# Gate and up projections: the low part of every second weight block made by an accumulating transfer instead of VectorE

## The chip, the cores and the metric

One core of one Trainium2 chip runs the whole program. The metric is the device time of one execution in microseconds (us). Lower is better.

## The reference, cut to what matters

The program is a decoder of two layers in float32 on 256 tokens of width 2048. Each layer has a mixer (retention and block attention) and a feed-forward part. The change touches only the first line of the feed-forward part and its product with the up projection:

```python
def conv_ffn(h, w_gate, w_up, conv_w, conv_b, w_down):
    a = h @ w_gate                       # 256 x 2048 times 2048 x 5632
    ...
    for j in range(CONV_WIDTH):
        conv = conv + conv_w[j] * a_pad[:, j:j + S]
    return (jax.nn.silu(conv) * (h @ w_up)) @ w_down
```

Everything is float32 outside and the result must keep that precision, so a product of two float32 matrices is made from parts: each operand is split into a high part (rounded to the type float32r that TensorE takes) and a low part (what the rounding left, again in float32r), and the products high by high, high by low and low by high are added up in PSUM.

## The kernel before, in words

All weights of both layers (428 MB) are read once, as a stream of 816 blocks, in a fixed order written out by hand (`units`). A block is 512 KB: two row tiles of 128 rows by 512 columns (or one row tile by 1024 columns). Each block goes through three steps.

- `load(i)` (line 552) has SyncE's queue (SP) bring the block from HBM into a tile `wraw`, of which there are 4.
- `prepare(i)` (line 561) makes the two parts: ScalarE (ACT) copies `wraw` into `whi`, which rounds it (line 56), and then VectorE (DVE) subtracts `whi` from `wraw` into `wlo` (line 57). There are 3 tiles `whi` and 3 tiles `wlo`, used in turn: block i takes the tiles of block i-3.
- `multiply(i)` (line 567) has TensorE (PE) do the block's matmuls.

The main loop puts them in order on the engines: in round i it issues `load(i+3)`, `prepare(i+2)` and then `multiply(i)`, and after that the small steps that are due (`slots`). Since the instructions of an engine run in the order in which they are issued, ACT's copy for block i+2 stands before the small steps of round i and after those of round i-1.

A block of the gate or up projection has the mode `ws4`. It is 8 pairs of matmuls, for two row tiles and four groups of 128 columns: the high part of the weights with both parts of the activations (512 columns, line 597), and the low part of the weights with the high part of the activations (256 columns, line 598). So the low part is wanted by the second matmul of a block. There are 176 such blocks in each layer, 8 to a chunk of 512 columns, gate and up chunks in turn. The small steps beside them are the convolution's taps and the gated product (`ffn_gate`, `ffn_up`): ACT, DVE and GpSimd (POOL) each have a few, the only ones on POOL being `sr` (line 463) and a tiny memset (line 448).

The other transfers that POOL's queue issues in the kernel are small parameters at the start and `dec` (line 236), a table of 768 KB, once in each layer.

Of the kernel before, what the change touches and what calls it, by code (L numbers as in the profile page):

```python
# [12 lines left out]
AF = mybir.ActivationFunctionType  # L13
OP = mybir.AluOpType
AX = mybir.AxisListType

P = 128
# [9 lines left out]
NC = 512  # L27
UK = 2
# [5 lines left out]
def trunk(ctx, tc, x, ln1_g, w_in, ret_norm_g, q_norm_g, k_norm_g, w_out, ln2_g,  # L34
          w_gate, w_up, conv_w, conv_b, w_down, decay, dneg, out):
    nc = tc.nc
    pe, act, dve, pool = nc.tensor, nc.scalar, nc.vector, nc.gpsimd
# [12 lines left out]
    def f(ap):  # L50
        return ap.bitcast(F32)

    def split(hi, lo, src, scale=None):
        """hi + lo == src * scale exactly, each in the tensor engine's float32r."""
        if scale is None:
            act.activation(hi, src, AF.Copy)  # L56
            dve.tensor_tensor(lo, src, f(hi), op=OP.subtract)  # L57
        else:
            act.activation(hi, src, AF.Copy, scale=scale)
            dve.scalar_tensor_tensor(lo, src, scale, f(hi), op0=OP.mult, op1=OP.subtract)  # L60
# [9 lines left out]
        pe.matmul(o, a_hi, b_lo, start=False, stop=False, **kw)  # L70
        pe.matmul(o, a_lo, b_hi, start=False, stop=last, **kw)  # L71

    # ---- constants, parameters by feature on the partitions
    xs = const.tile([P, 2, D], F32, name="xs")
    ident = const.tile([P, P], F32, name="ident")
    make_identity(nc, ident)
# [2 lines left out]
    rows = [[] for _ in range(6)]  # L79
# [33 lines left out]
    def pcol(t, at):  # L113
        return par[:, t, at:at + 1]

    # ---- the stream of weight blocks: UK tiles of 128 rows, 512 columns
    units = []
    slots = {}
    pre = {}
# [6 lines left out]
        slots.setdefault(i, []).append((fn, a))  # L126

    def chunk(w, col, kts, lhs, mode, done):
        """kts: pairs (row tile of w, key of lhs); lhs(key) -> [P, 2, 256] hi and lo."""
        box = {}  # L130
        n = len(kts)
        step = 1 if mode == "wm2" else UK
        for u in range(0, n, step):
            units.append((w, kts[u][0], col, lhs, [k for _, k in kts[u:u + step]], mode,
                          box, u == 0, u + step >= n, done))
# [11 lines left out]
    def g_of(k):  # L147
        return gT["t"][:, k]

    # ---- norm of x by 512 columns: transposed and split, the row factor left to later  # L150
    def finalize(c, l, which):
        add, last = fin_acc.pop("acc", None), l == L
        cs = slice(c * NC, (c + 1) * NC)
        if add is not None:
            for t in range(2):
                dve.tensor_tensor(xs[:, t, cs], add[t], xs[:, t, cs], op=OP.add)
                if last:
                    nc.sync.dma_start(xout[:, t, cs], xs[:, t, cs])
        if last:
            return  # L160
        for t in range(2):
            act.activation(junk, xs[:, t, cs], AF.Square, accum_out=ssx[:, t, c:c + 1])
# [22 lines left out]
    row = {}  # L185
# [37 lines left out]
                        norm_tail(l, which)  # L223
        return fn

    # ---- attention
    A = {}

    def open_attention():
# [11 lines left out]
    def moba_qk(l, hc, which):  # L241
        def fn(acc):
# [29 lines left out]
            def turn():  # L272
                T = A["p"].tile([P, 4, 2, S], F32R, tag=f"{which}T", name=f"{which}T")
                A[which, "T"] = T
                g = pcol(5, (gq_at if which == "q" else gk_at) + l)
                for b in range(2):
                    pt = bank().rearrange("p (k t) -> p k t", k=2)
                    for hh in range(2):
                        for t in range(2):
                            pe.transpose(pt[:, hh, t * P:(t + 1) * P], raw[:, t, 2 * b + hh], ident)  # L280
                    split(T[:, 2 * b:2 * b + 2, 0], T[:, 2 * b:2 * b + 2, 1], pt, g)
# [6 lines left out]
    def v_done(key):  # L288
        def fn(acc):
            v = A["p"].tile([P, 2, 2, NC], F32R, tag=key, name=key)  # L290
            A[key] = v
            for t in range(2):
                split(v[:, t, 0], v[:, t, 1], acc[t], row["r"][:, t:t + 1])
        return fn
# [125 lines left out]
        split_all([(y[:, 2 * h + kk, 0], y[:, 2 * h + kk, 1], pt[:, kk], pcol(5, gr_at + 8 * l + 2 * h + kk))  # L420
                   for kk in range(2)])

    # ---- feed-forward
    FFN = {}

    def open_ffn():
# [75 lines left out]
                later(i, tile_of, i)  # L502
        return fn

    # ---- the order of it all
    kd = [(k, k) for k in range(KD)]
    for l in range(L):
        b = len(units)
# [4 lines left out]
        for hc in range(2):  # L513
            o = hc * NC
            chunk(W, MQ + o, kd, h_of, "wm", moba_qk(l, hc, "q"))
            chunk(W, MK + o, kd, h_of, "wm", moba_qk(l, hc, "k"))
            chunk(W, MV + o, kd, h_of, "wm", v_done("mv"))
            chunk(W, RK + o, kd, h_of, "ws2", ret_qk("rk"))
            chunk(W, RQ + o, kd, h_of, "ws2", ret_qk("rq"))
            chunk(W, RV + o, kd, h_of, "wm", v_done("rv"))  # L520
            chunk(W, RG + o, kd, h_of, "wm", gate_done)
            for i in range(4):
                at_unit(b + (3 + 7 * hc) * U + 2 + 6 * i, moba_head, 4 * hc + i)
            e = b + (6 + 7 * hc) * U
            for i in range(2):
                h = 2 * hc + i
                at_unit(e + 1 + 3 * i, ret_scores, h)
                at_unit(e + 3 + 3 * i, ret_values, h)
                at_unit(e + 8 + 2 * i, ret_gate, h)
                at_unit(e + 9 + 2 * i, ret_turn, l, h)  # L530
# [19 lines left out]
    raws, parts = {}, {}  # L550
# [10 lines left out]
    def prepare(i):  # L561
        hi = wpool.tile([P, UK, NC], F32R, tag="whi", name="whi")
        lo = wpool.tile([P, UK, NC], F32R, tag="wlo", name="wlo")
        split(hi, lo, raws.pop(i))
        parts[i] = hi, lo

    def multiply(i):
# [39 lines left out]
    n = len(units)  # L607
# [11 lines left out]
    params([0])  # L619
    transposed(0, 0, 1)  # L620
    prepare(0)
    transposed(1, 0, 1)
    prepared = 1
# [11 lines left out]
    for i in range(n):  # L635
        now[0] = i
        for fn in pre.get(i, []):
            fn()
        load_to(i + 4)
        while prepared < min(n, i + 3):  # L640
            prepare(prepared)
            prepared += 1
        multiply(i)
        for fn, a in slots.pop(i, []):
            fn(*a)
# [46 lines left out]
```

## Time and profile before

| what | value |
| --- | --- |
| median time | 2386.4 us (2 runs, 2386.07 to 2386.74) |
| span of the profiled execution | 2387.3 us |
| PE busy | 2371.1 us (99%) |
| DVE busy | 1439.0 us (60%) |
| ACT busy | 1160.7 us (49%) |
| POOL busy | 179.9 us (8%) |
| moved by DMA | 436.14 MB, 183 GB/s over the span |

The span runs from the first to the last instruction of one execution. For the profiled execution no other time is recorded than its span; it is 0.9 us (0.04%) above the median of the unprofiled runs, and so the two are taken as one. Busy time is the time in which at least one instruction of the engine ran. Matmuls overlap, so a busy PE isn't a PE at its peak.

### The profile page before, as it was taken

The page shows a single profiled execution, that of the slowest core. Times are in us where ns is not written, and L with a number is a line of the kernel's source. Part 1 is how long each engine was busy: PE and PEld are TensorE (multiplying, and loading weights), DVE is VectorE, ACT ScalarE, POOL GpSimd, SP SyncE. Part 2 cuts the span into 40 slices and gives each one's busy share as a digit, 9 for nine tenths or more (in the row PEclk, how much of TensorE's full clock was granted, in tenths as well). Part 3 has the DMA queues.
Part 4 walks back from the last instruction along what each step waited for, and adds up shares of the span by engine and source line. Part 5 has one row for each costly group of instructions (what it writes and reads, how often), then busy time and mean ns, then how long its engine had stood idle before and what let it go on. Part 6 is the DMA issues. An engine that isn't in the chain of part 4 may idle for free.

```text
span 2387.3 us, 32695 instructions
## 1 busy us (share of the span) xinstructions
PE 2371.1 (99%) x12610; PEld 2025.1 (85%) x12610; DVE 1439.0 (60%) x1874; ACT 1160.7 (49%) x1616; POOL 179.9 (8%) x256
## 2 busy tenths in 40 slices
PE   9999999999999999999999999999999999999999
PEld 7988988888888888888889879888888888888777
DVE  5655655576676676444465565556767767774444
ACT  5445445455555555344354544445555555553333
POOL 2001000011011011000010010000101101100000
PEclk9999999999999999999999999999999999999999
DMA  7555555666666666555565565556666666665554
GB/s 241 168 168 174 177 162 177 184 186 187 190 183 191 187 184 193 186 184 186 187 187 177 159 179 167 170 182 183 187 187 187 190 188 187 187 191 187 192 181 148
DMA packets 199980, 436.14 MB, mean 183 GB/s; under 512 B 13506, under 2 KB 13634, under 8 KB 199824
## 3 DMA queue, kind: packets, MB, share of 16 engines
q1 hardware_dynamic: 199104, 432.07, 59.2%
q8 instruction: 98, 1.61, 0.3%
q0 software_dynamic: 672, 1.98, 0.2%
q14 instruction: 58, 0.48, 0.1%
q10 hardware_dynamic: 48, 0.02, 0.0%
HBM read 431.91 MB, written 2.10 MB: 182 GB/s over the span
## 4 chain that ended last, share of the span: by engine, by line
PE 97%; DVE 1%; POOL 1%; DMA 1%; ACT 0%; issue 0%; SPq 0%; ACTq 0%; POOLq 0%
PE bank L597 27%; PE bank L70 15%; PE bank L71 15%; PE bank L69 15%; PE bank L598 14%; PE bank L601 3%; PE bank L603 3%; PE bank L602 3%; PE bank L180 1%; DMA wraw<-in_w_down_dram 0%; POOL fac L257 0%; DVE wlo L57 0%; POOL sq L248 0%; PE bank L280 0%; DMA xs<-in_x_dram 0%; DVE raw L269 0%
## 5 line engine op out<-in xcount | busy, mean ns | idle before, releaser
L57 DVE TENSOR_TENSOR wlo<-wraw,whi 128x1024 fp32r<-128x1024 f32 x816 | 1009.9, 1238 | 778.0 <-ACT whi L56 775.1
L56 ACT ACTIVATE whi<-wraw 128x1024 fp32r<-128x1024 f32 x816 | 863.1, 1059 | 924.9 <-PE bank L71 460.5
L597 PE MATMUL bank<-h,whi 128*128 128x512 f32 x2816 | 989.6, 394 | 0.0
L598 PE MATMUL bank<-h,wlo 128*128 128x256 f32 x2816 | 796.5, 283 | 0.0
L597 PEld LDWEIGHTS bank<-h,whi 128*128 128x128 f32 x2816 | 528.8, 188 | 121.9
L598 PEld LDWEIGHTS bank<-h,wlo 128*128 128x128 f32 x2816 | 529.4, 188 | 0.1
L69 PE MATMUL bank<-whi,gT 128*128 128x512 f32 x704 | 279.8, 397 | 1.7 <-ACT whi L56 1.7
L70 PE MATMUL bank<-wlo,gT 128*128 128x512 f32 x704 | 279.7, 397 | 1.5 <-DVE wlo L57 1.5
L71 PE MATMUL bank<-whi,gT 128*128 128x512 f32 x704 | 279.4, 397 | 0.0
L69 PE MATMUL bank<-whi,h 128*128 128x512 f32 x640 | 255.9, 400 | 0.0
L70 PE MATMUL bank<-wlo,h 128*128 128x512 f32 x640 | 252.9, 395 | 0.0
L71 PE MATMUL bank<-whi,h 128*128 128x512 f32 x640 | 252.9, 395 | 0.0
L463 POOL TENSOR_TENSOR sr<-cv,rb 128x256 f32<-128x256 f32 x88 | 106.4, 1209 | 869.4 <-ACT cv L462 869.4
L69 PEld LDWEIGHTS bank<-whi,gT 128*128 128x128 f32 x704 | 132.9, 189 | 34.5 <-ACT whi L56 2.6
L70 PEld LDWEIGHTS bank<-wlo,gT 128*128 128x128 f32 x704 | 132.9, 189 | 34.3 <-DVE wlo L57 2.1
L71 PEld LDWEIGHTS bank<-whi,gT 128*128 128x128 f32 x704 | 133.0, 189 | 32.4
L601 PE MATMUL bank<-h,whi 128*128 128x256 f32 x512 | 145.2, 284 | 0.0
L71 PEld LDWEIGHTS bank<-whi,h 128*128 128x128 f32 x640 | 120.5, 188 | 28.5
L603 PE MATMUL bank<-h,wlo 128*128 128x256 f32 x512 | 144.2, 282 | 0.0
L602 PE MATMUL bank<-h,whi 128*128 128x256 f32 x512 | 144.0, 281 | 0.0
L70 PEld LDWEIGHTS bank<-wlo,h 128*128 128x128 f32 x640 | 120.8, 189 | 26.5 <-DVE wlo L57 0.3
L69 PEld LDWEIGHTS bank<-whi,h 128*128 128x128 f32 x640 | 120.8, 189 | 26.2
(132 smaller groups left out, 1885.1 us busy)
## 6 DMA issues: line engine op xcount, KB each, us to landing
wraw<-in_w_in_dram SPq DMA_DIRECT2D x224, 512.0 KB, 3.8
wraw<-in_w_gate_dram SPq DMA_DIRECT2D x176, 512.0 KB, 4.0
wraw<-in_w_up_dram SPq DMA_DIRECT2D x176, 512.0 KB, 4.3
wraw<-in_w_down_dram SPq DMA_DIRECT2D x176, 512.0 KB, 3.6
wraw<-in_w_out_dram SPq DMA_DIRECT2D x64, 512.0 KB, 3.6
xs<-in_x_dram SPq DMA_DIRECT2D x4, 512.0 KB, 6.7
out_dram<-xs SPq DMA_DIRECT2D x8, 256.0 KB, 3.7
dec<-in_decay_dram POOLq DMA_DIRECT2D x2, 768.0 KB, 5.6
```

The costliest lines, as they stand in the source:

```text
L56: act.activation(hi, src, AF.Copy)
L57: dve.tensor_tensor(lo, src, f(hi), op=OP.subtract)
L69: pe.matmul(o, a_hi, b_hi, start=first, stop=False, **kw)
L70: pe.matmul(o, a_hi, b_lo, start=False, stop=False, **kw)
L71: pe.matmul(o, a_lo, b_hi, start=False, stop=last, **kw)
L180: pe.transpose(pt[:, kk, t * P:(t + 1) * P], xs[:, t, cs + k * P:cs + (k + 1) * P], ident)
L463: pool.tensor_tensor(sr[:, i], cv, row["rb"], op=OP.mult)
L597: pe.matmul(acc[c], hi[:, j, cs], a, start=st, stop=False)
L598: pe.matmul(acc[c][:, :S], lo[:, j, cs], a[:, 0], start=False, stop=sp)
L601: pe.matmul(o, hi[:, j, cs], a[:, 0], start=st and c % 2 == 0, stop=False, skip_group_check=True)
L602: pe.matmul(o, hi[:, j, cs], a[:, 1], start=False, stop=False, skip_group_check=True)
L603: pe.matmul(o, lo[:, j, cs], a[:, 0], start=False, stop=sp, skip_group_check=True)
```

## The change

For the blocks of gate and up (mode `ws4`) with an odd index, `prepare` no longer calls `split`. ACT writes the negated, rounded copy of the block into `wlo`. POOL's queue then issues a transfer of the same 512 KB block from HBM that is added onto what stands in `wlo`, so that `wlo` holds the block less its rounded copy. After that ACT makes `whi` as before. DVE has no part in such a block. The block is thus read from HBM twice, by SP's queue into `wraw` and by POOL's into `wlo`.

```diff
     def prepare(i):
         hi = wpool.tile([P, UK, NC], F32R, tag="whi", name="whi")
         lo = wpool.tile([P, UK, NC], F32R, tag="wlo", name="wlo")
-        split(hi, lo, raws.pop(i))
+        w, k, col = units[i][:3]
+        if units[i][5] == "ws4" and i % 2:
+            raw = raws.pop(i)
+            act.activation(lo, raw, AF.Copy, scale=-1.0)
+            nc.gpsimd.dma_start(lo, w[k * P:(k + UK) * P, col:col + NC].rearrange("(k p) n -> p k n", p=P),
+                                accum_op=OP.add)
+            act.activation(hi, raw, AF.Copy)
+        else:
+            split(hi, lo, raws.pop(i))
         parts[i] = hi, lo
```

The rest of the diff empties some lines of comments and changes no instruction.

## Rows read from the trace of the kernel before

**Rows 1.** The page's busy times: engine, us, share of the span, instructions.

```profile
PE 2371.1 (99%) x12610; PEld 2025.1 (85%) x12610; DVE 1439.0 (60%) x1874; ACT 1160.7 (49%) x1616; POOL 179.9 (8%) x256
```

**Rows 2.** The page's chain of work that ended last, by engine.

```profile
PE 97%; DVE 1%; POOL 1%; DMA 1%; ACT 0%; issue 0%; SPq 0%; ACTq 0%; POOLq 0%
```

**Rows 3.** One line's matmuls (L597) in each layer: ns min/median/max, first and last start.

```profile
L597 PE MATMUL bank<-h,whi x1408: 387/396/484, 450.0 to 946.0; 128*128 128x512 f32 x176
L597 PE MATMUL bank<-h,whi x1408: 387/396/484, 1633.1 to 2129.0; 128*128 128x512 f32 x176
```

**Rows 4.** Groups by line, 460 to 920 us: busy, mean ns, idle before and its releasers.

```profile
L57 DVE TENSOR_TENSOR wlo<-wraw,whi 128x1024 fp32r<-128x1024 f32 x165 | 206.8, 1253 | 130.5 <-ACT whi L56 130.5
L56 ACT ACTIVATE whi<-wraw 128x1024 fp32r<-128x1024 f32 x164 | 173.9, 1060 | 186.6 <-PE bank L597 112.3 <-issue 63.2 <-ACT cv L455 9.9
L463 POOL TENSOR_TENSOR sr<-cv,rb 128x256 f32<-128x256 f32 x40 | 48.6, 1215 | 394.4 <-ACT cv L462 394.4
```

**Rows 5.** Timeline around one block's end: start, us, engine, operation, idle before.

```profile
716.12 1.06 ACT L56 ACTIVATE whi<-wraw 128x1024 fp32r<-128x1024 f32 x1 [0.82 <-PE bank L597]
...
718.45 0.40 PE L597 MATMUL bank<-h,whi 128*128 128x512 f32 x1
718.68 0.28 PE L598 MATMUL bank<-h,wlo 128*128 128x256 f32 x1
718.80 0.39 PE L597 MATMUL bank<-h,whi 128*128 128x512 f32 x1
718.93 1.06 ACT L56 ACTIVATE whi<-wraw 128x1024 fp32r<-128x1024 f32 x1 [1.10 <-PE bank L597]
719.03 0.28 PE L598 MATMUL bank<-h,wlo 128*128 128x256 f32 x1
```

**Rows 6.** Timeline of ACT, then of POOL: ACT's end releases POOL.

```profile
708.65 0.40 ACT L462 ACTIVATE cv<-cv 128x256 f32<-128x256 f32 x1
...
709.14 1.51 POOL L463 TENSOR_TENSOR sr<-cv,rb 128x256 f32<-128x256 f32 x1 [34.83 <-ACT cv L462]
```

**Rows 7.** The page's DMA issues: queue, count, KB each, median us to landing.

```profile
wraw<-in_w_gate_dram SPq DMA_DIRECT2D x176, 512.0 KB, 4.0
wraw<-in_w_up_dram SPq DMA_DIRECT2D x176, 512.0 KB, 4.3
dec<-in_decay_dram POOLq DMA_DIRECT2D x2, 768.0 KB, 5.6
stage<-in_ln_g_dram ACTq DMA_DIRECT2D x1, 16.0 KB, 3.0
stage<-in_ln_g_dram POOLq DMA_DIRECT2D x1, 16.0 KB, 5.6
stage<-in_k_norm_g_dram POOLq DMA_DIRECT2D x1, 1.0 KB, 5.1
```

**Rows 8.** The tile dec alone: issue on POOL, and us from issue to landing.

```profile
L236 POOL DMA_DIRECT2D dec<-in_decay_dram x2: 593/615/637, 30.6 to 1199.0; - x2
...
DMA to landing us min/median/max: 4.8/5.6/6.5
```

**Rows 9.** Windows: us, engines' busy times (count), PEclk, DMA share, GB/s.

```profile
10.00:20.00 10.00, 10.00 (x45) 8.04 (x45) 7.15 (x12) 8.19 (x19) 0.00 (x0) 1.00 1.04 377
...
1850.00:2100.00 250.00, 250.00 (x1426) 219.10 (x1425) 176.78 (x246) 134.55 (x201) 28.23 (x47) 1.00 0.65 188
```

**Rows 10.** The chain of work, 2255 us on: a late transfer's piece and what it released.

```profile
2255.17 5.67 DMA wraw<-in_w_down_dram
2260.94 1.06 ACT whi L56
```

**Rows 11.** Timeline of PE behind that: the waits, then slower matmuls.

```profile
2262.05 0.50 PE L69 MATMUL bank<-whi,gT 128*128 128x512 f32 x1 [0.89 <-ACT whi L56]
2263.31 0.50 PE L70 MATMUL bank<-wlo,gT 128*128 128x512 f32 x1 [0.76 <-DVE wlo L57]
...
2266.32 0.63 PE L70 MATMUL bank<-wlo,gT 128*128 128x512 f32 x1
2266.75 0.63 PE L71 MATMUL bank<-whi,gT 128*128 128x512 f32 x1
...
2268.92 0.39 PE L69 MATMUL bank<-whi,gT 128*128 128x512 f32 x1
2269.15 0.40 PE L70 MATMUL bank<-wlo,gT 128*128 128x512 f32 x1
```

**Rows 12.** The granted clock there: windows with the columns of rows 9.

```profile
2265.00:2266.00 1.00, 1.00 (x4) 0.77 (x3) 0.95 (x1) 0.00 (x0) 0.00 (x0) 0.50 1.00 309
2269.00:2270.00 1.00, 1.00 (x6) 0.82 (x5) 0.73 (x1) 0.00 (x0) 0.00 (x0) 1.00 0.60 231
```

## The prediction, made before the result was known

> **What bounds the kernel now.** Read the busy times first: PE is busy for 2371.1 of 2387.3 us, so only 16 us of the span are free of matmuls [rows 1]. Then the chain of work that ended last: 97% of it is PE, DVE has 1% [rows 2]. An engine that prepares blocks faster has nothing to give here. Next the pace in the stage that the change touches: from the first to the last line-597 matmul of a layer 496.0 us pass with 1408 pairs, thus 1407 steps, in both layers alike [rows 3]; 496.0 / 1407 x 8 = 2.82 us for a block, 5.64 for two, 2 x 176 x 2.82 = 993 us in all. Last the two preparing engines in that stage: DVE's subtraction takes 1.25 us of the 2.82 and waits for ACT before it; ACT's copy takes 1.06, and most of its idle time ends with a matmul that frees a tile `whi` [rows 4]. So both are ahead of PE, held back by the 3 tiles alone.
>
> **What sets how late a low part may come.** Block u takes the tiles of block u-3 and is issued in round u-2. Nothing can be written into its `wlo` before the last line-598 matmul of u-3 ends; call that E. In the trace such an end is 718.68 + 0.28 = 718.96 us, and the next block's first line-598 matmul starts at 719.03 [rows 5]. Block u's first use of `wlo` comes two blocks later, at E + 0.07 + 5.64 = E + 5.71. That is the allowance. Before, the path through it was 0.08 + 1.06 + about 0.04 + 1.25 = 2.4 us.
>
> **The change part by part.**
>
> Removed: one subtraction for each odd block of gate and up, 88 in each layer, 176 x 1.25 = 220 us of DVE [rows 4]. PE's work hides all of it: 0 us.
>
> Added on ACT: 176 x 1.06 = 187 us of a second copy. ACT has 1060 + 187 of 2387 us then. The copy to `whi` now stands behind the negated one and ends at about E + 0.08 + 2.12 = E + 2.2, wanted at about E + 5.5: hidden by 3.3 us of PE's work. The negated copy waits for line 598's last matmul and not line 597's, 0.11 us later [rows 5]; queued behind it on ACT are the `whi` copy and the small steps of the round, whose results are wanted a round or more later: 0.
>
> Added on POOL: one DMA issue for each odd block, behind a wait for ACT. Queued behind it on POOL are `sr` and the memset. `sr` takes 1.2 us, waits for most of its time on ACT [rows 4], and is read by the up chunk that follows: 0. SP's queue is passed by nothing new; it waits for ACT's `whi` copy instead of DVE for the odd blocks. A tile `wraw` is free at about E + 2.2 and its next block wanted at E + 4 x 2.82, 9.1 us later; a load takes 4.0 to 4.3 us [rows 7], so it has almost 5 us to spare: 0.
>
> Added to the path: the low part now goes ACT, POOL, transfer, PE. Step by step from E: 0.08 until ACT starts, as behind line 597 [rows 5]; 1.06 copy; 0.09 from ACT's end (708.65 + 0.40) to POOL's start [rows 6]; then L, from POOL's issue to landing; 0.10 from landing (2255.17 + 5.67) to the engine that waits [rows 10]. Sum L + 1.33. Since the allowance is 5.71, PE waits as soon as **L is over 4.38 us**.
>
> What one wait costs: with D = L + 1.33 - 5.71, the first odd block comes D late. The next odd block's tile was freed before that wait, so its transfer ran during it, and the wait of one is taken off the next one's. Two odd blocks in a row wait D together, whether as D and 0 or as two halves. The cost is 176 x D / 2 = **88 x D**.
>
> What L is: no accumulating transfer stands in the trace. Nearest rows, from below: a plain load of the same block from SP's queue lands in 4.0 to 4.3 us [rows 7]; as the floor that gives no wait at all. From POOL's queue 768 KB (`dec`) landed in 4.8 and 6.5 us, the longer one with several loads beside it [rows 8]. The 16 KB of `stage` took 3.0 us from ACT's queue and 5.6 from POOL's, and even 1 KB took 5.1 [rows 7] (those queued behind others at the start), so POOL's queue has a long fixed part. The DMA engines at full load move 377 GB/s [rows 9]; at that rate the 786 KB of `dec` are 2.1 us, which leaves 2.7 to 4.4 us fixed. An addition must read both the block and what lies in the tile, 2 x 524 KB, or 2.8 us at that rate: L = 5.5 to 7.2. The loads already keep the DMA engines busy for 0.65 of the stage [rows 9], so the loaded end is nearer: I take **L = 7.0**, D = 2.62, 88 x 2.62 = 231 us. From above: if the second read also doubles the data's time, 4.4 + 2 x 2.8 = 10.0 us.
>
> The clock on top. The trace has a place where a transfer came late: PE stood 0.89 and 0.76 us within two matmuls, and from about 1.5 us later the matmuls of 512 columns started 0.43 us apart rather than 0.23, for 8 matmuls; the granted clock was 0.50 (1.2 GHz), and 1.00 (2.4 GHz) again behind it [rows 11, 12]. That is 8 x 0.20 = 1.6 us lost for a halt of about that size. The first odd block of the stage waits the whole D and the second nothing, so the halts are about 2.6 us in each four blocks, longer than those two together. If each brought the clock down, that were 88 x 1.6 = 141 us; if the halts spread into halves, none. I take 0.6 of it, 83 us.
>
> Sum: 2387.3 + 231 + 83 = **2701 us**. The median of the runs is 0.9 us below that span, which I leave aside.
>
> **Where the Trainium skill bears on it.** `dec` has 4.8 and 6.5 us for 768 KB [rows 8]. The Trainium skill, "DMA: Bandwidth & Descriptors", section "Anatomy of one DMA — SWDGE (gpsimd) path", gives for a transfer from this queue some 2.0 us and the bytes at 436 GB/s, an estimate of 3.2 us for our block, under which nothing would wait; by it `dec` should take 3.8, so this trace disagrees with it beside other traffic. The Trainium skill, "Collectives: The Full Stack", section "The bandwidth ceiling: the fold count and why AG ≠ RS ≠ AR", says that an addition in the transfer path halves the rate because it needs two source reads; no run here shows it yet, and it stands with the two reads that I count above.
>
> **The rivals.**
>
> (a) *The transfer is hidden after all* (not slower). One mechanism: the addition lands in under 4.38 us, as SP's loads of the same size do, because most of the 5.1 us of the small transfers was queueing at the start. Then PE sees nothing: 2387 us. For it, the 4.8 us of one `dec` with half as much data again; at L = 4.8, D = 0.42 and the time is 2387 + 37 = 2424. Against it, the 6.5 of the other and the second read.
>
> (b) *The addition is far slower than two reads at full rate*, because a DMA engine that reads, adds and writes back goes through its rows one after another. Each additional microsecond of L is 88 us. At L = 10, D = 5.62, 495 us and the clock's 141: 3023. At L = 15 some 3460 to 3600. Then the DMA engines, not the wait for one transfer, may set the pace and the loads come late too. Nothing in the trace speaks for or against it; the 0.65 busy share leaves 2 of 5.64 us in two blocks for the third transfer, where a plain one takes 0.65 x 2.82 = 1.8.
>
> (c) *Only the waits, no clock*: the halts spread evenly, 1.3 us in each pair of blocks, and the clock stays at 1.00 as it does in this stage now [rows 9]: 2387 + 231 = 2618. With the full price of the clock it is 2759.
>
> (d) *The change does less than it says*: DVE is relieved and gains something. There is no room for it: even all of PE's idle time is 16 us, 0.7%.
>
> **How the numbers follow.** The forecast's mechanism (L between 4.9 and 9, with or without the clock) has 0.78: from 2387 + 88 x 0.52 = 2433 to 2387 + 88 x 4.62 + 141 = 2935. In it L between 5.6 and 9 has 0.70, from 2495 up. Rival (a) has 0.08, rival (b) beyond L = 9 has 0.13, (d) 0.01. (c) and the full clock are in the forecast's range. For 8 in 10 I go a little past both ends of the forecast's core, 2470 to 2970. Within 2% means up to 2434 us; 2% is about what a measurement here can tell from no change. Rival (a) makes "same" 0.08, a gain of over 2% has 0.01, the rest, 0.91, is slower.
>
> **What the changed profile would show.** Right: in gate and up PE idles before line 598, released by a DMA on `wlo`, up to 176 times and in total near 88 x D; the chain of work shows that DMA; POOL's queue has 176 issues of 512 KB with a landing time of 6 to 8 us; DVE's busy time falls by 220 us and ACT's rises by 187; the rest of the program keeps its times; the granted clock falls behind the long halts. Wrong: landing under 4.4 us and no waits (rival a); landing at 10 us or more, or a DMA share near 1 with ACT waiting for `wraw` (rival b); PE waiting for `whi` rather than `wlo`, which would mean that ACT's second copy is on the path after all. The step that I trust least is L.

## The result, and the profile after

The changed kernel takes 2822.7 us (median of 2 runs, 2813.1 to 2832.2) against 2386.4: 1.183 times as long, interval 1.173 to 1.192. The forecast was 2701 us with a range of 2470 to 2970 and a chance of 0.91 for slower. The profiled execution is the run of 2832.2 us; its span is 2830.5.

The busy times of the changed kernel, from the page, answer to [rows 1]:

```profile
PE 2519.4 (89%) x12610; PEld 2121.7 (75%) x12610; DVE 1221.8 (43%) x1698; ACT 1314.7 (46%) x1792; POOL 387.3 (14%) x432
```

PE does the same 12610 matmuls, but is busy for 148.3 us more (2519.4 less 2371.1), and its idle time has grown from 16.2 to 311.1 us, by 294.9. The two make the whole difference of the spans, 443.2 us. So the first question is why PE stands, and the second why the same matmuls take longer.

The chain of work that ended last, by engine, answers to [rows 2]:

```profile
PE 62%; DMA 18%; issue 11%; ACT 3%; POOL 3%; DVE 3%; SPq 0%; POOLq 0%; DVEq 0%; ACTq 0%
```

DMA had 1% of the chain and has 18%. What PE waited for (engine, line, releaser: us in total, times, longest), the two largest rows:

```profile
PE bank L606 <- DMA wlo<-in_w_up_dram: 147.2, 51, 5.3
PE bank L606 <- DMA wlo<-in_w_gate_dram: 146.9, 51, 4.6
```

Nearly all of the new idle time, 294.1 of 294.9 us, ends with an adding transfer that lands, at line 606, the low part's matmul (line 598 before). Two rows of DMA issues, with the landing times, and the line's first and last matmuls in each layer, which answer to [rows 7] and [rows 3]:

```profile
wlo<-in_w_gate_dram POOLq DMA_DIRECT2D x88, 512.0 KB, 7.7
wlo<-in_w_up_dram POOLq DMA_DIRECT2D x88, 512.0 KB, 7.7
```

```profile
L605 PE MATMUL bank<-h,whi x1408: 387/396/633, 451.0 to 1162.6; 128*128 128x512 f32 x176
L605 PE MATMUL bank<-h,whi x1408: 387/396/633, 1849.7 to 2573.3; 128*128 128x512 f32 x176
```

The stage takes 711.6 and 723.6 us where it took 496.0 twice: 443.2 more, so nothing was lost outside it. One late block in the timeline (start, us, engine, line, operation; idle before and its releaser):

```profile
705.55 0.28 PE L606 MATMUL bank<-h,wlo 128*128 128x256 f32 x1
...
705.87 1.06 ACT L567 ACTIVATE wlo<-wraw 128x1024 fp32r<-128x1024 f32 x1 [1.96 <-PE bank L606]
...
706.83 1.04 ACT L570 ACTIVATE whi<-wraw 128x1024 fp32r<-128x1024 f32 x1
...
707.22 1.20 POOL L568 DMA_DIRECT2D wlo<-in_w_gate_dram  x1 [1.77 <-ACT wlo L567]
...
711.29 0.39 PE L605 MATMUL bank<-h,whi 128*128 128x512 f32 x1
714.68 0.58 PE L606 MATMUL bank<-h,wlo 128*128 128x256 f32 x1 [3.00 <-DMA wlo<-in_w_gate_dram]
715.06 0.63 PE L605 MATMUL bank<-h,whi 128*128 128x512 f32 x1
```

The block that frees the tile ends at 705.83. ACT starts 0.04 us later, POOL issues 0.29 us after ACT's end at 706.93, this transfer lands 7.4 us after its issue, and PE goes on at 714.68: 8.85 us from the freed tile to the first use, against an allowance of 5.71. PE stood 3.00 us. From there on the matmuls are longer: the high one takes 0.63 where it took 0.39. The granted clock of a stretch before the halt and one behind it (columns as in [rows 9]):

```profile
708.00:711.00 3.00, 3.00 (x19) 2.64 (x18) 1.31 (x2) 1.48 (x3) 0.43 (x1) 1.00 0.63 129
715.00:720.00 5.00, 5.00 (x17) 4.22 (x17) 0.00 (x0) 0.39 (x1) 0.00 (x0) 0.50 0.99 234
```

It is 1.00 (2.4 GHz) before and 0.50 (1.2 GHz) for 5 us behind. POOL's issues show the rhythm:

```profile
724.29 1.20 POOL L568 DMA_DIRECT2D wlo<-in_w_gate_dram  x1 [10.25 <-ACT wlo L567]
729.91 1.20 POOL L568 DMA_DIRECT2D wlo<-in_w_gate_dram  x1 [4.42 <-ACT wlo L567]
741.43 1.20 POOL L568 DMA_DIRECT2D wlo<-in_w_up_dram  x1 [10.33 <-ACT wlo L567]
747.04 1.20 POOL L568 DMA_DIRECT2D wlo<-in_w_up_dram  x1 [4.27 <-ACT wlo L567]
```

They come 5.6 and 11.5 us apart in turn: two blocks at full pace are 5.64, so here one odd block waits and the next one doesn't. In the whole run 102 of the 176 low parts are waited for, 2.9 us on average.

### The profile page after: what moved, and what is told of

It reads as the page before. It is cut to its first block, busy times and chain, and to the rows that moved or that the text cites. A ratio compares the mean times of both kernels' runs of the same rounds, so it can differ in the third digit from the quotient of the medians.

```text
span 2830.5 us, 33030 instructions
## 1 busy us (share of the span) xinstructions
PE 2519.4 (89%) x12610; PEld 2121.7 (75%) x12610; DVE 1221.8 (43%) x1698; ACT 1314.7 (46%) x1792; POOL 387.3 (14%) x432
## 3 DMA queue, kind: packets, MB, share of 16 engines
q0 software_dynamic: 48544, 94.26, 18.4%
## 4 chain that ended last, share of the span: by engine, by line
PE 62%; DMA 18%; issue 11%; ACT 3%; POOL 3%; DVE 3%; SPq 0%; POOLq 0%; DVEq 0%; ACTq 0%
PE bank L70 13%; PE bank L71 13%; PE bank L69 13%; PE bank L605 10%; DMA wlo<-in_w_up_dram 9%; DMA wlo<-in_w_gate_dram 8%; PE bank L606 6%; PE bank L609 2%; PE bank L611 2%; PE bank L610 2%; ACT wlo L567 2%; POOL wlo L568 1%; DVE wlo L57 1%; POOL sr L463 1%; ACT whi L56 1%
## 5 line engine op out<-in xcount | busy, mean ns | idle before, releaser
L57 DVE TENSOR_TENSOR wlo<-wraw,whi 128x1024 fp32r<-128x1024 f32 x640 | 783.6, 1225 | 1421.5 <-ACT whi L56 1418.8
L606 PE MATMUL bank<-h,wlo 128*128 128x256 f32 x2816 | 863.7, 307 | 294.3 <-DMA wlo<-in_w_up_dram 147.2
L605 PE MATMUL bank<-h,whi 128*128 128x512 f32 x2816 | 1105.4, 427 | 0.0
L606 PEld LDWEIGHTS bank<-h,wlo 128*128 128x128 f32 x2816 | 589.7, 209 | 330.0 <-DMA wlo<-in_w_up_dram 165.2
L605 PEld LDWEIGHTS bank<-h,whi 128*128 128x128 f32 x2816 | 587.9, 209 | 138.2
L567 ACT ACTIVATE wlo<-wraw 128x1024 fp32r<-128x1024 f32 x176 | 186.3, 1059 | 259.2 <-PE bank L606 256.2
L568 POOL DMA_DIRECT2D wlo<-in_w_gate_dram x88 | 105.8, 1203 | 649.3 <-ACT wlo L567 447.0
L568 POOL DMA_DIRECT2D wlo<-in_w_up_dram x88 | 105.8, 1202 | 478.8 <-ACT wlo L567 473.7
L611 PE MATMUL bank<-h,wlo 128*128 128x256 f32 x512 | 144.2, 282 | 0.0
```

The lines of the kernel that those rows point to most:

```text
L567: act.activation(lo, raw, AF.Copy, scale=-1.0)
L568: nc.gpsimd.dma_start(lo, w[k * P:(k + UK) * P, col:col + NC].rearrange("(k p) n -> p k n", p=P), accum_op=OP.add)
L605: pe.matmul(acc[c], hi[:, j, cs], a, start=st, stop=False)
L606: pe.matmul(acc[c][:, :S], lo[:, j, cs], a[:, 0], start=False, stop=sp)
L611: pe.matmul(o, lo[:, j, cs], a[:, 0], start=False, stop=sp, skip_group_check=True)
```

## The experiments

The theory: the loss is 88 x D, D being the time by which an addition lands past the allowance, and on top a low clock that follows from the halts. The rivals were that the load on the DMA engines or on POOL's queue costs something for each transfer, and that the low clock has another cause.

**every_fourth: half as many adding transfers.**

```diff
-        if units[i][5] == "ws4" and i % 2:
+        if units[i][5] == "ws4" and i % 4 == 1:
```

> Edit: only every fourth gate and up block (index 1 modulo 4) has its low part made by the adding transfer, 88 in all and not 176; the others go through VectorE. Theory (a late transfer costs one halt D, and the next odd block is free because its transfer ran during that halt, so two odd blocks cost D together): halving the number of transfers saves next to nothing, 2780 to 2830 us, with 88 halts of about 3.3 us before the low part's matmul. Rival (each transfer costs its own share, by load on the DMA engines, POOL or ACT): half of the loss goes, 2387 + 218 = 2605 us.

Measured: 2781.4 us, 1.165 times before (1.161 to 1.168). With 88 transfers and not 176 the loss falls by a tenth, from 436 to 395 us. What PE waited for:

```profile
PE bank L606 <- DMA wlo<-in_w_up_dram: 141.5, 44, 5.1
PE bank L606 <- DMA wlo<-in_w_gate_dram: 136.4, 44, 4.4
```

88 halts, 278 us, 3.16 each: one for each of these blocks. The rival's 2605 falls. In the changed kernel every second transfer was nearly free: the 88 that it has more cost 41 us together.

**four_tiles: the same transfers, issued one block earlier.**

```diff
+    def prepare_low(i):                 # called in round i-3
+        if i < n and units[i][5] == "ws4" and i % 2:
+            lo = lows[i] = wpool.tile([P, UK, NC], F32R, tag="wlo", name="wlo", bufs=4)
+            act.activation(lo, raws[i], AF.Copy, scale=-1.0)
+            nc.gpsimd.dma_start(lo, ..., accum_op=OP.add)
...
-            z = A["w"].tile([P, 2, S], F32, tag="z", name="z")
+            z = A["p"].tile([P, 2, S], F32, tag="sq", name="z")
-            sr = w.tile([P, 4, S], F32, tag="sr", name="sr")
+            sr = w.tile([P, 4, S], F32, tag="sr", name="sr", bufs=1)
```

> Edit: four tiles for low parts, and the negated copy and the adding transfer of an odd block issued one round earlier (three blocks ahead of its use and not two); high parts as before. To make room, sr has one buffer and the tile z takes the place of sq. Theory (only the time from a freed tile to the landed addition counts, about 9.2 us): the allowance grows from 5.71 to 8.53 us, D is 0.7 us, 88 x 0.7 = 60 us: 2430 to 2480 us, with landing still 7.5 to 8 us. Rival (the DMA engines or POOL's queue can't carry three 512 KB transfers in two blocks, so the pace is set by throughput): the landing time grows with the pressure and the time stays over 2650 us.

Measured: 2402.0 us, 1.007 times before (1.004 to 1.010). All 176 transfers are there. Windows of 500 to 900 us, of four_tiles and then of the changed kernel (columns as in [rows 9]):

```profile
500.00:900.00 400.00, 399.80 (x2273) 349.33 (x2272) 193.41 (x324) 278.53 (x391) 126.32 (x143) 1.00 1.05 280
```

```profile
500.00:900.00 400.00, 319.65 (x1579) 270.70 (x1578) 135.14 (x222) 191.24 (x272) 90.90 (x100) 0.89 0.81 196
```

The DMA engines move 280 GB/s here against 196 in the changed kernel and 188 before [rows 9], and PE hardly stands. So throughput isn't what held the changed kernel back; the time from the freed tile to the use is. With a DMA share of 1.05 there is nothing to spare, though. The time lies below the 2430 to 2480 us that the theory gave. The landing time shrank to 6.6 us, better than the 7.5 to 8 expected, for a reason that no run here shows. With the allowance of 8.53 that leaves next to no wait: PE waits 8.8 us in all for these transfers. The kernel is still no faster than before, since PE set the pace already.

**no_add_pool: the same transfer without the addition.**

```diff
-            nc.gpsimd.dma_start(lo, w[...].rearrange(...), accum_op=OP.add)
+            nc.gpsimd.dma_start(lo, w[...].rearrange(...))
```

> Edit: the transfer on POOL's queue copies the block into the low tile and adds nothing (the low part is then the whole block, so the subtraction is left out of the computation); order, sizes and waits are those of the changed kernel. Theory (the addition's second read and write back is what makes the landing 7.7 us): it lands in 5.5 to 6 us as the table dec does, D is about 1.5 us, 2500 to 2560 us. Rival (the fixed part of POOL's queue and its 1.2 us of issue make it, whatever the transfer does): it lands in 7 us or more, 2700 us or more.

Measured: 2481.0 us, 1.039 times before (1.028 to 1.050). The issue on POOL and the time from issue to landing (ns min/median/max; us min/median/max), then the same of the changed kernel:

```profile
L568 POOL DMA_DIRECT2D wlo<-in_w_gate_dram x88: 713/716/810, 448.6 to 2202.4; - x88
...
DMA to landing us min/median/max: 3.8/4.1/8.4
```

```profile
L568 POOL DMA_DIRECT2D wlo<-in_w_gate_dram x88: 1193/1198/1300, 449.5 to 2527.6; - x88
...
DMA to landing us min/median/max: 7.1/7.7/9.9
```

A plain copy from POOL's queue lands in 4.1 us, faster than the theory said and as fast as SP's loads (4.5 in this run): the addition costs 3.6 us, 0.48 of them in the issue. The time, too, lies below the 2500 to 2560 us of the theory. With a median of 4.1 no wait would be expected; the 72 us of halts come from 48 that landed late (up to 8.4 us). The rival, a queue that is slow whatever it carries, falls. A smaller part stays: without any addition the second transfer of these blocks still costs 95 of the 436 us, so not the whole loss is the addition's.

**half_add: only half of the rows are added.**

```diff
-            nc.gpsimd.dma_start(lo, w[k * P:(k + UK) * P, col:col + NC].rearrange(...), accum_op=OP.add)
+            nc.gpsimd.dma_start(lo[:, 0], w[k * P:(k + 1) * P, col:col + NC], accum_op=OP.add)
```

> Edit: the adding transfer brings only the first of the block's two row tiles (256 KB, 128 rows of 2 KB); the other half of the low part stays the negated copy, so that half of the correction is left out of the computation. Copies, order and waits are as in the changed kernel. Theory (what an addition costs over the plain transfer's 4.1 us grows with the rows: 3.6 us for 256 rows): landing at about 5 us, issue at 0.8 us and not 1.2, D about 0.7, 2440 to 2500 us. Rival (an addition has a fixed delay, before its first row or behind its last): landing at 6.5 us or more, 2650 us or more.

Measured: 2444.2 us, 1.024 times before (1.022 to 1.026); landing 4.6 us, issue 0.86 us. As the theory said, there is no large fixed delay: 128 rows more, with 256 KB more, cost 3.1 us of landing (7.7 less 4.6).

**long_rows: the same bytes in half as many rows.**

```diff
-            nc.gpsimd.dma_start(lo, w[k * P:(k + UK) * P, col:col + NC].rearrange(...), accum_op=OP.add)
+            c2 = min(col, FF - UK * NC)
+            nc.gpsimd.dma_start(lo.rearrange("p k n -> p (k n)"), w[k * P:(k + 1) * P, c2:c2 + UK * NC], accum_op=OP.add)
```

> Edit: the adding transfer brings as many bytes (512 KB) in 128 rows of 4 KB and not 256 rows of 2 KB, from one row tile and 1024 columns; what is added is then another part of the weights, so the low part's values are left wrong, while copies, order and waits are those of the changed kernel. half_add landed in 4.6 us and the full addition in 7.7, so 128 more rows of 2 KB cost 3.1 us. Theory (that price is per byte: each engine reads, reads again and writes every byte): landing at 7 to 8 us, 2750 to 2850 us. Rival (the price is per row: an engine goes through its rows one after another, each with a delay of its own): landing near half_add's, 4.6 to 5.5 us, 2440 to 2520 us.

Measured: 2640.5 us, 1.106 times before (1.097 to 1.115); landing 6.4 us, issue 0.86. Neither side: taken at face value, of the 3.1 us that separate half_add from the full addition 1.3 go with the number of rows (0.34 of that is the issue) and 1.8 with the bytes. Only the part of the issue is firm. SP's loads took 5.3 and 6.1 us here against 4.4 in the changed kernel, and the landing of one and the same addition differs between the runs by more than 1.3 us (6.6 in four_tiles, 9.2 in filler), so the rest of the split isn't shown.

**high_first: the low part used later in the block.**

```diff
+        if mode == "ws4" and i % 2:
+            for part in range(2):
+                ...                    # part 0: the 8 high matmuls, part 1: the 8 low ones
```

> Edit: in odd gate and up blocks all 8 high matmuls come before the 8 low ones, so that the low part is first used 7 x 0.21 = 1.5 us later; nothing else. Theory (88 x D, D the landing past the allowance, and a clock loss that shrinks with the halts): D falls from 3.4 to about 1.9 us, 88 x 1.9 = 167 us of halts and 0 to 100 us of slow matmuls: 2560 to 2660 us. Rival (PE's order inside a block doesn't matter, since what counts is when tiles come free, and those come free at the block's end as before): 2800 us as in the changed kernel.

Measured: 2674.7 us, 1.121 times before (1.112 to 1.129; its 2 runs are 2657.8 and 2691.6). PE's waits:

```profile
PE bank L608 <- DMA wlo<-in_w_gate_dram: 93.8, 61, 4.1
PE bank L608 <- DMA wlo<-in_w_up_dram: 89.7, 52, 4.1
```

1.5 us of later use took 148 us off the time. The halts came to 183.5 us where 167 were expected, with a landing of 7.9 us, and the total is 15 us above the range given (one of its runs lies in it). The rival's 2800 falls.

**filler: work in place of the halts.**

```diff
                     pe.matmul(acc[c], hi[:, j, cs], a, start=st, stop=False)
+                    if i % 2 and j == 0 and c == 0:
+                        for _ in range(16):
+                            pe.matmul(acc[c][:, :S], hi[:, j, cs], zero, start=False, stop=False)
```

> Edit: in each odd gate and up block TensorE does 16 more matmuls of 256 columns with a moving operand of zeros, between the first high and the first low matmul: 176 x 16 x 0.118 = 332 us of added work, 1.9 us for a block, that adds exactly 0 to the result. Theory (of the loss of about 443 us some 305 are halts and some 120 to 140 are matmuls at 1.2 GHz that follow from halts of over 3 us): the added work fills the halts, the granted clock stays near 1.00, and the kernel is faster than the changed one in spite of it: 2387 + 332 = 2720 us, up to 2750. Rival (the low clock has another cause, or costs nothing of its own): filling takes the place of the halts and the clock's share stays, 2830 to 2860 us.

Measured: 2875.0 us, 1.204 times before (1.200 to 1.207), where theory said 2720 to 2750 and the rival 2830 to 2860. The clock did come back (0.990 over the span, against 0.947), but the landing time of the additions rose to a median of 9.2 us, and 104 us of halts stayed. The time proves neither side.

**filler_fourth: the same where the transfers stand alone.** The edit, against that of filler:

```diff
-        if units[i][5] == "ws4" and i % 2:
+        if units[i][5] == "ws4" and i % 4 == 1:
...
-                    if i % 2 and j == 0 and c == 0:
-                        for _ in range(16):
+                    if i % 4 == 1 and j == 0 and c == 0:
+                        for _ in range(26):
```

> Edit: as every_fourth, and in each of those 88 blocks 26 more matmuls of 256 columns with a moving operand of zeros (about 3.1 us, adding exactly 0) between the first high and the first low matmul. In every_fourth 88 halts make 278 us and some 110 us more come from matmuls at 1.2 GHz. Theory (the low clock follows from the halts): TensorE never stands, the clock stays at 1.00, and only the filled time is left, 2387 + 88 x 3.1 = 2660 to 2690 us, about 100 us faster than every_fourth with 2288 more matmuls. Rival (the 110 us are no consequence of the halts): 2770 us or more. If the landing time of the adding transfers grows by more than 0.5 us against 7.5, as it did in filler, the run decides only by its granted clock.

Measured: 2711.4 us, 1.136 times before (1.134 to 1.138), 70 us faster than every_fourth with 2288 matmuls more. That is 21 us above the theory's range and 59 below the rival's. The landing time stayed at 7.6 us, so the comparison holds. The busy times, first of every_fourth and then of filler_fourth:

```profile
PE 2481.6 (89%) x12610; PEld 2095.0 (75%) x12610; DVE 1339.0 (48%) x1786; ACT 1227.8 (44%) x1704; POOL 294.9 (11%) x344
```

```profile
PE 2666.4 (98%) x14898; PEld 2305.5 (85%) x14898; DVE 1346.2 (50%) x1787; ACT 1228.1 (45%) x1704; POOL 295.3 (11%) x344
```

In every_fourth the matmuls of the kernel take 110.5 us more than before (2481.6 less 2371.1), at a granted clock of 0.961 over the span; some 14 us of that are waits that a running matmul hides (88 x 0.16, see below). With the halts filled it is 0.999. A filled block shows 3.33 us between the end of its first high matmul's turn (712.73) and the first low one (716.06), a bit more than the 3.1 planned; 88 x 3.3 = 293 and 22 us of halts that remain are 315 of the 320 us by which the span exceeds that of before. That the low clock follows from the halts, and costs time of its own, is shown by this pair.

## Why the prediction was right, and where its sizes were off

**The bound and the allowance.** Right. The preparing engines had nothing to give (DVE lost 217 us of work and PE gained nothing), and PE waits where it was said, at the low part's matmul, for the transfer. four_tiles and high_first move the allowance from either end, and the time follows.

**88 x D.** Right, and every_fourth shows the odd part of it: two odd blocks in a row wait D together, so half of the transfers cost next to nothing. With the median landing of 7.7 us and the path's other steps as the trace has them (8.85 less 7.4 = 1.45 us; the forecast had 1.33), D = 7.7 + 1.45 - 5.71 = 3.44 and 88 x D = 303 us; 294 were measured as idle time. A wait is a little longer than the idle time that it leaves, since the matmul before it is still running: the low matmul above was due 0.23 us after 711.29, the usual step [rows 5], and came 3.16 us late, while PE counts as idle for 3.00. For 102 waits that is some 16 us, so the waits cost about 310.

**L, the term that was mis-sized first.** The forecast took 7.0 us; 7.7 were measured, 62 us of the difference at 88 us for each. That it came so near is luck: two errors partly cancel. POOL's queue was taken to have a fixed part of 2.7 to 4.4 us, from `dec`'s 4.8 and 6.5, and L = 7.0 counts 4.2 for it (7.0 less 2.8); the plain copy's 4.1 us for the whole block, less 1.4 for its bytes at the forecast's rate, leaves 2.7, or 1.5 less. And the second read was taken to cost 1.4 us at full rate; the addition costs 3.6, or 2.2 more. Of a price for each row, which rival (b) was about, the runs show only the 0.34 us of long_rows, and in POOL's issue; whether the DMA engines have one stays open.

In engine time an addition is dearer by less: the queue's page rows, of the changed kernel, of no_add_pool and of long_rows (packets, MB, share of 16 engines' span):

```profile
q0 software_dynamic: 48544, 94.26, 18.4%
```

```profile
q0 software_dynamic: 48544, 94.26, 14.4%
```

```profile
q0 software_dynamic: 26016, 94.26, 21.3%
```

18.4% of 2830.5 us against 14.4% of 2490.0, 521 against 359 us for the same bytes, 1.45 times. In long_rows it is 21.3% of 2647.3, 564 us: half as many rows didn't make the engines' part cheaper. The Trainium skill, "Collectives: The Full Stack", section "The bandwidth ceiling: the fold count and why AG ≠ RS ≠ AR", has ReduceScatter, which adds, at half the rate of AllGather, which copies, because the add needs two source reads; it says so of collectives in a ring. The direction agrees here: an addition takes 1.45 times as long in engine time and 1.9 times in landing. The Trainium skill, "DMA: Bandwidth & Descriptors", section "Anatomy of one DMA — SWDGE (gpsimd) path", gives an estimate of 3.2 us for a transfer of this size. The plain copy took 4.1 beside the loads, and what was added took 7.7.

**The clock, the other term that was mis-sized.** 83 us were forecast. PE's busy time grew by 148, of which some 16 are the hidden ends of waits, so the clock took about 130. That busy time grows without the clock too shows in half_add, where PE is busy for 24.6 us longer than before (2395.7 less 2371.1) at a granted clock of 0.999. The clock records of the trace fit that: 67 stretches at 0.50 (3 before), 303 us in all, in which at most 151 us of matmul time can be lost, and less where PE stood. The forecast knew from one place that a halt brings the matmuls to 1.2 GHz for 1.6 us of loss, and counted that for six of ten halts. Both were too low: about 130 us over 67 stretches are some 2.0 us for each, and 67 are 0.76 of 88. The stretch shown above stays at 0.50 for over 5 us, longer than the 8 matmuls of [rows 11], so the 1.6 us was no upper bound for one halt.

The two terms together, 294 + 148 = 442, against the forecast's 231 + 83 = 314, are the whole miss; with the hidden ends counted as waits they are about 310 and 130.

**Rival (a)** failed by 3.3 us of landing. **Rival (c)**, even halts without a loss of clock, didn't occur: the issues come 5.6 and 11.5 us apart, and the granted clock fell. **The covers** held: PE shows no wait for the second ACT copy in this stage, and none for `sr` or the memset on POOL. SP's loads land in 4.4 us and not 4.0 to 4.3, inside their 5 us to spare. ACT's busy time rose by 154 us and not 187: its second copy starts 0.10 us before the first one ends (706.83 against 706.93), which covers some 18 of the 33.

## What to carry to other kernels

Before an engine's pass is moved into a transfer, count from the moment when the destination tile comes free to the first use: a transfer that lands inside that time costs next to nothing (16 us for 176 of them in four_tiles), and one that lands past it costs the bottleneck engine directly, even where the DMA engines have time to spare (a share of 0.81 in the changed kernel). If it is late, issue it earlier (one more tile and one round took away nearly all of this loss) or use its result later in the block. And when the bottleneck engine is PE, a halt can cost more than its own length: the halt of 3.00 us shown above was followed by 5 us at 0.50, while half_add's halts, 0.5 us on average and 1.8 at most, left the granted clock at 0.999 over the span.

## What the runs showed of the hardware that was not expected

An adding transfer of 512 KB lands in 7.7 us where a plain one from the same queue takes 4.1, and its issue on POOL takes 1.20 us against 0.72.

The landing time of the same addition differs with the schedule around it: 6.6 us in four_tiles, 7.7 in the changed kernel and 9.2 in filler. The load on the DMA engines doesn't explain the order: their share between 500 and 900 us is 1.05, 0.81 and 0.81. SP's loads beside the additions land in 6.2, 4.4 and 4.7 to 5.3 us. It may be that the two kinds of transfers take time from each other, and that the order in which they start decides which one pays. No run moved the loads alone, so this stays open.

TensorE finished sooner with more to do: 2288 useless matmuls in the halts of every_fourth made that kernel 70 us faster. It still takes 324 us more than before.
